# Layer trunk on one core: first norm's squares from token rows, six more low parts by DMA sums, a wrapper around the mixer's small loads

## The chip, the core and the metric

The kernel runs on one core of a Trainium2 chip. A core has a matrix engine (TensorE: PE for the matmuls, PEld for the loads of their weights), VectorE (DVE), ScalarE (ACT), GpSimd (POOL) and a queue engine (SP) that issues most transfers; 16 DMA engines carry them. The metric is the device time of one execution in microseconds (us), the median of several runs; lower is better.

## The reference

Two layers on 512 tokens of width 1024, float32. The part that the change touches is the very first feed-forward block and the first norm ahead of it:

```python
def rms_norm(x, g):
    xf = x.astype(jnp.float32)
    y = xf * lax.rsqrt(jnp.mean(xf * xf, axis=-1, keepdims=True) + EPS) * g.astype(jnp.float32)
    return y.astype(x.dtype)

def swiglu(h, w_gate, w_up, w_down):
    return (jax.nn.silu(h @ w_gate) * (h @ w_up)) @ w_down

    for l in range(DEPTH):
        x = x + 0.5 * swiglu(rms_norm(x, ffn_norm[l, 0]), ffn_w_gate[l, 0], ffn_w_up[l, 0], ffn_w_down[l, 0])
        h = rms_norm(x, mix_norm[l])
        ...
        x = x + m
        x = x + 0.5 * swiglu(rms_norm(x, ffn_norm[l, 1]), ffn_w_gate[l, 1], ffn_w_up[l, 1], ffn_w_down[l, 1])
    return x
```

The mixer of layer 0 is a Mamba-2 and mLSTM block, that of layer 1 sparse attention. The mixer's small vectors (`hy_dt_bias`, `hy_a_log`, `hy_d_skip` and two gate biases) are parameters of layer 0's mixer.

## The kernel before, in words

Every float32 matmul is done as three matmuls (`mm3`, L280 to L282): each operand is split into a high part and a low part (the rest), and high x high, high x low and low x high are summed. For a weight block of 128x1024 (half a megabyte, a `raw` buffer), the split is called a form: ACT copies the high part into a `form` buffer (L468), DVE subtracts it from the raw block to give the low part (L470). There are 4 raw buffers and 5 form buffers, taken in a ring; a raw buffer is loaded again once both parts are made, a form buffer is written again once the matmuls that read it are done. `both(...)` has a second way, `summed`: ACT writes the negative of the high part where the low part belongs (L497), POOL issues a transfer that adds the raw block to it (L498, a DMA sum), and ACT copies the high part (L499). It is in use elsewhere in the kernel.

The kernel starts with `load_x`: x is loaded token by row in four parts (`xin`), interleaved on SP with the four weight blocks of the first unit (two of `w_gate`, two of `w_up`). PE transposes x into features by row (L355, tile `pxt`), DVE copies it out (L362), and `prep_later` makes from each feature chunk of 128x512 the split and scaled `xgn` (ACT L753, DVE L756), its square (ACT L765) and the running sum of squares `ssq` (POOL L463). At the end of the chunks the sum over features is 24 matmuls with one column (`sums`, L401, tile `pssq`), then DVE L729 and POOL L731 give the norm's factor per token (`rcol`), four transposes (L422, tile `prow`) turn it into a row, and ACT L735 writes `rrow`.

The feed-forward block goes in units of 256 hidden features. The first two (`unit`, `EIGHT` = 2) compute gate (`pg`) and up (`pu`) from `xgn` in two passes over the four forms of the unit (features 0 to 3, then 4 to 7: 12 matmuls for each form and pass), and apply `rrow` on the way out (DVE L463 `ft<-pg`). Meanwhile `xforms` builds from x and `rrow` (DVE L550) seven combined forms of x (`xf`); the later units use these in a seven-product scheme (`unit_seven`, tiles `pA`, `pD`, `pB`). `settle_later` places the two steps of the norm's factor in the first unit.

The steps of a stage are recorded in a `Plan` with a cost each; `Plan.order` sorts them, and they are issued in that order on each engine. Code outside the plan (the whole mixer of layer 0, `hybrid` with `gates`) is ordered by the framework's own scheduler, which may issue instructions ahead that have nothing to wait for. `tc.issue_after(ins)` keeps what is written in its block, on the engine of `ins`, behind `ins` in that engine's order. `self.mark` is a DVE instruction (the low part L756 of a norm's first chunk).

Of the kernel before, what the change touches and what calls it, by code (L numbers as in the profile page):

```python
# [10 lines left out]
F32 = mybir.dt.float32  # L11
F32R = mybir.dt.float32r
AF = mybir.ActivationFunctionType
ALU = mybir.AluOpType
AX = mybir.AxisListType

P = 128
T = 512
NB = T // P
D = 1024  # L20
KC = D // P
FF = 2816
EPS = 1e-6
# [190 lines left out]
class Trunk:  # L214
# [121 lines left out]
    def load_x(self, which, ahead):  # L336


        nc = self.nc
        xin = [Lazy(lambda: self.part.tile([P, 2, NB, 256], F32, name="xin", tag="xin")) for i in range(2)]  # L340
        first = []
        for i in range(4):
            cols = self.a["x"][0, :, i * 256 : (i + 1) * 256].rearrange("(b p) n -> p b n", p=P)
            self.plan.add(
                "sync", 1.7, lambda i=i, cols=cols: nc.sync.dma_start(xin[i // 2]()[:, i % 2], cols), (), [("xin", i)], 3.2
            )
            first.append(self.block(ahead[i // 2], i % 2))

        def chunks():
            for k in range(KC):  # L350
                pt = Lazy(lambda: self.mmps("pxt"))

                def turn(k=k, pt=pt):
                    for b in range(NB):
                        nc.tensor.transpose(  # L355
                            pt()[:, b * P : (b + 1) * P],
                            xin[k // 4]()[:, (k // 2) % 2, b, (k % 2) * P : (k % 2 + 1) * P],
                            self.ident,
                        )

                self.t(0.5, turn, [("xin", k // 2)], [("pxt", k)])
                self.v(T, lambda k=k, pt=pt: nc.vector.tensor_copy(self.xT[:, k], pt()), [("pxt", k)], self.xk(k))  # L362
                if k % 2:
                    self.prep_later(which, k - 1, k == KC - 1)
                    yield

        return first, chunks()

    def split_gain(self, hi, lo, src, g):
# [87 lines left out]
    def t(self, us, issue, reads, writes):  # L457
        self.plan.add("tensor", us, issue, reads, writes)
# [220 lines left out]
        self.seven(raws, xf, False, ((g2, g2k), (one, onek), (two, twok)), (c11, c12, c21, c22))  # L679
        return t, tk  # L680

    def unit(self, raws, stream, late):


        nc, rrow = self.nc, self.rrow
        ps = self.pair("pg", "pA"), self.pair("pu", "pB")
        f = []
        for qs in ((0, 1), (2, 3)):
            for i in range(4):
                for _ in range(2 if not f else 1):  # L690
                    next(stream, None)
                xg, xgk = self.xg, self.xgk
                if len(f) < 4:
                    f.append(self.made(raws[i]))
                j, b = f[i]
                for s in range(2):
                    col = slice(s * P, (s + 1) * P)
                    for q in qs:
                        k = 2 * q + i % 2
                        self.times(  # L700
                            *ps[i // 2], s, (j, lambda b=b, q=q, col=col: (b[:, 0, q, col], b[:, 1, q, col])),
                            lambda k=k: (xg[0][k], xg[1][k]), xgk(k), q == 0 and i % 2 == 0, q == 3 and i % 2 == 1, False, T,
                            0.693,
                        )
                if 2 * qs[0] + i in ((2, 4) if late else (1, 3)):
                    self.settle_later()
        yield
        t, tk = self.place()
        g = lambda: t()[:, 4:8].rearrange("p (s a) b -> p s (a b)", s=2)
        h = lambda: t()[:, 0:4].rearrange("p (s a) b -> p s (a b)", s=2)  # L710
        r = lambda: rrow.unsqueeze(1).to_broadcast([P, 2, T])
        gk, hk = ([tk(a + i) for i in range(4)] for a in (4, 0))
        pk = lambda ps: [(*ps[1], 0), (*ps[1], 1)]
        self.vtt(2 * T, g, ps[0][0], r, ALU.mult, gk, pk(ps[0]) + ["rrow"])
        self.s(2 * T, lambda: nc.scalar.activation(g(), g(), AF.Silu), gk, gk)  # L715
        self.vtt(2 * T, h, ps[1][0], r, ALU.mult, hk, pk(ps[1]) + ["rrow"])
        self.vtt(2 * T, h, h, g, ALU.mult, hk, hk + gk)
        yield t, tk
# [17 lines left out]
                   ["prow"], ["rrow"])  # L736
        self.pending = max(self.pending - 1, 0)

    def prep_later(self, which, k, last):

        nc = self.nc
        if k == 0:
            self.which = which
            self.xgn = [[Lazy(lambda: self.part.tile([P, 4, T], F32R, name="xgn", tag="xg")) for _ in range(2)] for _ in range(2)]
            self.ssqs, self.ssqk = [Lazy(lambda: self.tmp.tile([P, T], F32, name="ssq", tag="ssq", bufs=1))], ["ssq"]
            self.xg = [LazyFeat(t) for t in self.xgn]
            self.xgk = lambda k: [("xg", which, i, k) for i in range(2)]
        xgn, xT = self.xgn, self.xT
        for j in (k, k + 1):
            g, x = self.gain(which, j), xT[:, j]  # L750
            hi, lo = (lambda i=i, j=j: xgn[i][j // 4]()[:, j % 4] for i in range(2))
            hik, lok = ([("xg", which, i, j)] for i in range(2))
            self.s(T, lambda hi=hi, x=x, g=g: nc.scalar.activation(hi(), x, AF.Copy, scale=g), self.xk(j), hik)  # L753

            def low(hi=hi, lo=lo, x=x, g=g, j=j):
                ins = nc.vector.scalar_tensor_tensor(lo(), x, g, hi().bitcast(F32), op0=ALU.mult, op1=ALU.subtract)  # L756
                if j == 0:
                    self.mark = ins

            self.v(T, low, self.xk(j) + hik, lok)  # L760
            if j == 0:
                sq, sk = self.ssqs[0], ["ssq"]
            else:
                sq, sk = Lazy(lambda: self.tmp.tile([P, T], F32, name="sq", tag="t1")), [("sq", j % 2)]
            self.s(T, lambda x=x, sq=sq: nc.scalar.activation(sq(), x, AF.Square), self.xk(j), sk)  # L765
            if last:
                self.ssqs, self.ssqk = self.ssqs + [sq], self.ssqk + sk
            elif j:
                ssq = self.ssqs[0]
                self.vtt(T, ssq, ssq, sq, ALU.add, ["ssq"], ["ssq"] + sk, True)  # L770
        if last:
            self.pending = 2

    def ffn(self, l, i, nxt, first=(), stream=iter(())):

        a = self.a
        wg, wu, wd = (a[n][l, i] for n in ("ffn_w_gate", "ffn_w_up", "ffn_w_down"))
        xf, tiles = [], [Lazy(lambda: self.part.tile([P, 2, 4, H], F32R, name="xf", tag="xf", bufs=7)) for _ in range(7)]
        self.count["xf"] = self.count.get("xf", 0) + 1
        for u0, u1 in GROUPS:  # L780
            hid = []
            for u in range(u0, u1):
                col = slice(u * 256, u * 256 + 256)
                raws = first if first and not u else [self.block(w[:, col], par) for w in (wg, wu) for par in range(2)]
                if u < EIGHT:
                    made = self.unit(raws, stream, bool(first))
                    next(made)
                    xf += self.xforms(2 * u, tiles)
                    t, tk = next(made)
                else:  # L790
                    t, tk = self.unit_seven(raws, xf)
                hid.append(self.forms(t, tk))
            self.down(wd[u0 * 256 : u1 * 256], hid, u1 == UNITS, nxt)
# [251 lines left out]
    def gates(self, w, cols, g):  # L1045


        nc = self.nc
        a = self.a
# [2 lines left out]
            nc.sync.dma_start(raw[:, :, o : o + n], w[:, c : c + n].rearrange("(k p) n -> p k n", p=P))  # L1052

        vec = self.consts[:, 7, 72:120]
        for o, n, name in ((0, 16, "hy_dt_bias"), (16, 4, "hy_fgate_bias"), (20, 4, "hy_igate_bias"), (24, 16, "hy_a_log")):
            nc.sync.dma_start(vec[:, o : o + n], a[name].partition_broadcast(P))
        ds = a["hy_d_skip"].rearrange("e (c two) -> two (e c)", two=2)
        for h in range(2):
            nc.sync.dma_start(vec[h * 64 : (h + 1) * 64, 40:48], ds[h].partition_broadcast(64))
        gbias, nega, self.dskip = vec[:, 0:24], vec[:, 24:40], vec[:, 40:48]  # L1060
        nc.scalar.activation(nega, nega, AF.Exp)
        nc.vector.tensor_scalar(nega, nega, -1.0, None, op0=ALU.mult)
        f = self.form(raw)
# [12 lines left out]
        def st(name, n):  # L1076
            used[0] += NB * n
            return box[:, used[0] - NB * n : used[0]].rearrange("p (b n) -> p b n", b=NB)
# [8 lines left out]
        u, s, z, p = st("gu", 20), st("gs", 20), st("gz", 20), st("gp", 20)  # L1087
# [49 lines left out]
        ms, mx, mt, aa, wk, em = (st(n, 4) for n in ("gms", "gmx", "gmt", "gaa", "gwk", "gem"))  # L1137
# [684 lines left out]
```

## Time and profile before

| what | us |
|---|---|
| median of 3 runs | 2045.16 (2044.39 to 2046.2) |
| the profiled execution, its own time | 2046.62 |
| its span in the trace | 2044.9 |
| PE busy in the span | 2004.9 (98%) |
| DVE, ACT, POOL busy | 1590.7, 1165.3, 268.8 |

The profile was taken from one execution; times in it count from the start of the span. Its own time is 1.7 us more than the span, and 1.5 us above the median. PE's busy time counts a matmul from its start to a modelled end, so matmuls that follow each other overlap; what PE loses is read from the waits in brackets (`[idle before <-who released it]`) and from the distance between starts.

### The profile page before, as it was taken

How to read it: one execution, taken by the hardware profiler on the slowest of the kernel's cores; microseconds unless marked ns; L12 is line 12 of the kernel's file. 1: busy time of each engine (PE TensorE's matmuls, PEld its weight loads, DVE VectorE, ACT ScalarE, POOL GpSimd, SP SyncE). 2: the span in 40 equal slices, each digit the busy share in tenths (PEclk: the TensorE clock that was granted, in tenths of full speed). 3: DMA queues.
4: the chain of work that ended last, by engine and by line, in shares of the span. 5: the costliest groups of instructions: out<-in, count | busy, mean ns of one | idle time of the engine just before them, and what ended most of it. 6: DMA issues, size and time to landing. Idle time of an engine off the chain costs nothing.

```text
span 2044.9 us, 34611 instructions
## 1 busy us (share of the span) xinstructions
PE 2004.9 (98%) x14018; PEld 1818.9 (89%) x14018; DVE 1590.7 (78%) x2337; ACT 1165.3 (57%) x1695; POOL 268.8 (13%) x332
## 2 busy tenths in 40 slices
PE   7999999999999999999999999999998999999998
PEld 6899999787788888999998899999865667999998
DVE  5998878786537638989878898878678847988886
ACT  4666666442335534757566575756667544756665
POOL 2000001310001001000012010000214321000010
PEclk8999999999999999999999999999899999999999
DMA  4457566332221232656665356655654302566664
GB/s 155 104 157 174 154 159 145 124 93 73 67 78 61 75 102 64 155 152 169 154 162 148 93 150 162 169 156 144 157 137 89 73 5 78 137 164 160 159 164 116
DMA packets 210728, 257.60 MB, mean 126 GB/s; under 512 B 13708, under 2 KB 186888, under 8 KB 210568
## 3 DMA queue, kind: packets, MB, share of 16 engines
q1 hardware_dynamic: 190640, 185.58, 29.4%
q0 software_dynamic: 19728, 69.74, 18.2%
q8 instruction: 110, 1.80, 0.4%
q14 instruction: 50, 0.41, 0.1%
q10 hardware_dynamic: 200, 0.06, 0.0%
HBM read 183.53 MB, written 2.10 MB: 91 GB/s over the span
## 4 chain that ended last, share of the span: by engine, by line
PE 90%; DVE 5%; ACT 2%; DMA 1%; issue 1%; POOL 0%; ACTq 0%; DVEq 0%; POOLq 0%; SPq 0%
PE pA L281 10%; PE pA L280 10%; PE pA L282 10%; PE pD L281 5%; PE pD L280 5%; PE pD L282 5%; PE pB L281 3%; PE pB L280 3%; PE pB L282 3%; PE po L280 2%; PE po L282 2%; PE po L281 2%; PE pu L280 1%; PE ptok L280 1%; PE ptok L282 1%; PE ptok L281 1%
## 5 line engine op out<-in xcount | busy, mean ns | idle before, releaser
L470 DVE TENSOR_TENSOR form<-raw,form 128x1024 fp32r<-128x1024 f32 (+1 forms) x332 | 397.3, 1202 | 117.8 <-ACT form L468 116.8
L468 ACT ACTIVATE form<-raw 128x1024 fp32r<-128x1024 f32 (+1 forms) x332 | 339.5, 1028 | 189.9 <-DVE raw L463 120.5
L282 PE MATMUL pA<-xf,form 128*128 128x256 f32 x1152 | 322.2, 280 | 1.5 <-DVE form L470 1.5
L280 PE MATMUL pA<-xf,form 128*128 128x256 f32 x1152 | 322.4, 280 | 0.2 <-ACT ft L614 0.2
L281 PE MATMUL pA<-xf,form 128*128 128x256 f32 x1152 | 322.0, 280 | 0.0
L463 DVE TENSOR_TENSOR raw<-raw 128x1024 f32<-128x1024 f32 (+1 forms) x240 | 283.5, 1185 | 11.6 <-DMA raw<-in_ffn_w_up 5.1
L498 POOL DMA_DIRECT2D form<-raw x131 | 113.3, 865 | 1197.8 <-ACT form L497 1123.5
L282 PEld LDWEIGHTS pA<-xf,form 128*128 128x128 f32 x1152 | 216.4, 188 | 1.7 <-DVE form L470 1.7
L280 PEld LDWEIGHTS pA<-xf,form 128*128 128x128 f32 x1152 | 216.4, 188 | 0.5 <-ACT ft L614 0.4
L281 PEld LDWEIGHTS pA<-xf,form 128*128 128x128 f32 x1152 | 216.4, 188 | 0.2
L497 ACT ACTIVATE form<-raw 128x1024 fp32r<-128x1024 f32 (+1 forms) x131 | 135.1, 1031 | 139.9 <-PE pD L282 77.6
L281 PE MATMUL pA<-hid,form 128*128 128x256 f32 x704 | 198.6, 282 | 1.9 <-DVE hid L470 1.5
L280 PE MATMUL pA<-hid,form 128*128 128x256 f32 x704 | 198.1, 281 | 0.1
L282 PE MATMUL pA<-hid,form 128*128 128x256 f32 x704 | 196.9, 280 | 0.0
L282 PE MATMUL pD<-xf,form 128*128 128x256 f32 x576 | 161.2, 280 | 0.0
L280 PE MATMUL pD<-xf,form 128*128 128x256 f32 x576 | 161.2, 280 | 0.0
L281 PE MATMUL pD<-xf,form 128*128 128x256 f32 x576 | 161.1, 280 | 0.0
L463 DVE TENSOR_TENSOR ft<-ft 128x256 f32<-128x256 f32 (+2 forms) x288 | 146.2, 539 | 4.2 <-ACT ft L715 0.7
L281 PEld LDWEIGHTS pA<-hid,form 128*128 128x128 f32 x704 | 132.4, 188 | 3.7 <-DVE hid L470 3.7
L499 ACT ACTIVATE form<-raw 128x1024 fp32r<-128x1024 f32 (+1 forms) x131 | 133.6, 1021 | 0.0
L280 PEld LDWEIGHTS pA<-hid,form 128*128 128x128 f32 x704 | 132.4, 188 | 0.6 <-DVE ft L463 0.5
L282 PEld LDWEIGHTS pA<-hid,form 128*128 128x128 f32 x704 | 132.1, 188 | 0.0
(439 smaller groups left out, 5247.6 us busy)
## 6 DMA issues: line engine op xcount, KB each, us to landing
form<-raw POOLq DMA_DIRECT2D x115, 512.0 KB, 5.7
raw<-in_ffn_w_gate SPq DMA_DIRECT2D x88, 512.0 KB, 3.8
raw<-in_ffn_w_up SPq DMA_DIRECT2D x88, 512.0 KB, 3.7
raw<-in_ffn_w_down SPq DMA_DIRECT2D x64, 512.0 KB, 4.3
raw<-in_hy_w_in SPq DMA_DIRECT2D x44, 512.0 KB, 3.5
raw<-in_ffn_w_down SPq DMA_DIRECT2D x32, 384.0 KB, 3.4
raw<-in_hy_w_out SPq DMA_DIRECT2D x16, 512.0 KB, 3.3
form<-raw POOLq DMA_DIRECT2D x16, 384.0 KB, 4.1
```

What stands on the lines that cost most here:

```text
L280: mm(out, l[0], r[0], start=start, stop=False)
L281: mm(out, l[0], r[1], start=False, stop=False)
L282: mm(out, l[1], r[0], start=False, stop=stop)
L463: (self.p if pool else self.v)(n, lambda: e.tensor_tensor(out(), x(), y(), op=op), reads, writes)
L468: self.s(n, lambda: nc.scalar.activation(hi(), src(), AF.Copy), srck, hik)
L470: n, lambda: nc.vector.tensor_tensor(lo(), src(), hi().bitcast(F32), op=ALU.subtract), srck + hik, lok
L497: self.s(n, lambda: nc.scalar.activation(f()[:, 1], raw, AF.Copy, scale=-1.0), rawk, lok)
L498: self.plan.add("gpsimd", 0.85, lambda: nc.gpsimd.dma_start(f()[:, 1], raw, accum_op=ALU.add), rawk + lok, lok, 5.5)
L499: self.s(n, lambda: nc.scalar.activation(f()[:, 0], raw, AF.Copy), rawk, hik)
```

## The change

Three edits. First, in `load_x`, eight ACT instructions take the squares straight from the token rows `xin`, each with an accumulator that gives the sum over 512 features of 128 tokens; two DVE instructions of 4 columns and one on POOL give `rcol`. The first norm's `prep_later` makes no squares (`squares=False`) and leaves only the transposes of `rcol` to `settle_later` (`pending` 1 in place of 2). Second, of the first two units of the first block, forms 2 and 3 of unit 0 and all four of unit 1 are made with `summed`. Third, the six small loads in `gates` stand in a block `tc.issue_after(self.mark.ins)`.

```diff
+        act = nc.scalar.activation
+        part, (ms, rcol) = self.cols[:, 1], (self.cols[:, 0, i] for i in range(2))
+        self.turn, self.rcol = 1, rcol
+        for i in range(2):
+            for b in range(NB):
+                sq = Lazy(lambda: self.tmp.tile([P, T], F32, name="sq", tag="t1"))
+                self.s(T + 200, lambda i=i, b=b, sq=sq: act(
+                    sq().rearrange("p (i n) -> p i n", i=2), xin[i]()[:, :, b], AF.Square, accum_out=part[:, i, b : b + 1]
+                ), [("xin", 2 * i), ("xin", 2 * i + 1)], [("sq", b % 2), "part"])
+        self.vtt(4, lambda: ms, lambda: part[:, 0], lambda: part[:, 1], ALU.add, ["ms"], ["part"])
+        self.v(4, lambda: nc.vector.tensor_scalar(ms, ms, 1.0 / D, EPS, op0=ALU.mult, op1=ALU.add), ["ms"], ["ms"])
+        self.p(64, lambda: nc.gpsimd.tensor_tensor(rcol, ms, self.mhalf, op=ALU.pow), ["ms"], ["rcol"])
...
-                    self.prep_later(which, k - 1, k == KC - 1)
+                    self.prep_later(which, k - 1, k == KC - 1, False)
...
-                    f.append(self.made(raws[i]))
+                    f.append(self.made(raws[i], i >= summed))
...
+            if not squares:
+                continue
...
-            self.pending = 2
+            self.pending = 1 + squares
...
-                    made = self.unit(raws, stream, bool(first))
+                    made = self.unit(raws, stream, bool(first) and not u, 2 * (1 - u) if first else 4)
...
+        with self.tc.issue_after(self.mark.ins):
+            for o, n, name in ((0, 16, "hy_dt_bias"), (16, 4, "hy_fgate_bias"), (20, 4, "hy_igate_bias"), (24, 16, "hy_a_log")):
+                nc.sync.dma_start(vec[:, o : o + n], a[name].partition_broadcast(P))
```

Where the instructions stand, first on PE in unit 0, between the third and the fourth form's matmuls (`pu` is the up product, `pssq` the sums of squares, `prow` the transposed factor). Before:

```order
L282 MATMUL pu<-xgn,form 128x512
L401 MATMUL pssq<-raw,ssq 128x1 [waits Pool_49]
L401 MATMUL pssq<-raw,sq 128x1 [waits Activation_49] x2
L401 MATMUL pssq<-raw,ssq 128x1
...
L280 MATMUL pu<-xgn,form 128x512
L281 MATMUL pu<-xgn,form 128x512
L282 MATMUL pu<-xgn,form 128x512 [waits DVE_49]
```

and after:

```order
L282 MATMUL pu<-xgn,form 128x512
L435 MATMUL prow<-raw 128x128 [waits Pool_49]
L435 MATMUL prow<-raw 128x128 x3
L280 MATMUL pu<-xgn,form 128x512 [waits Activation_49]
L281 MATMUL pu<-xgn,form 128x512
L282 MATMUL pu<-xgn,form 128x512 [waits DMASW1_49]
```

The 24 matmuls on `pssq` are gone; the four transposes, which stood in the second pass, stand in their place, and the third matmul of the next form waits for a DMA sum (DMASW) and no longer for DVE.

On ACT, from the third and fourth form of unit 0 to the first form of unit 1 (L753 and L767 make `xgn`, L468 and L481 high parts, L510 the negatives for a sum, L512 high parts beside a sum, L765 and L355 the squares). Before:

```order
L468 ACTIVATE form<-raw 128x1024 [waits DMAHW7_49]
L468 ACTIVATE form<-raw 128x1024 [waits DMAHW1_49]
L1061 ACTIVATE raw<-raw 128x16 [waits DMAHW2_49]
L765 ACTIVATE sq<-raw 128x512 [waits DVE_49,Pool_49] x2
L753 ACTIVATE xgn<-raw 128x512 [waits DMAHW4_49,PE_49]
L753 ACTIVATE xgn<-raw 128x512
L468 ACTIVATE form<-raw 128x1024 [waits DMAHW0_49]
L765 ACTIVATE sq<-raw 128x512 [waits DVE_49,Pool_49]
L753 ACTIVATE xgn<-raw 128x512
L765 ACTIVATE sq<-raw 128x512 [waits DVE_49]
```

and after:

```order
L355 ACTIVATE sq,raw<-xin 128x512 x2
L510 ACTIVATE form<-raw 128x1024 [waits DMAHW0_49]
L512 ACTIVATE form<-raw 128x1024
L355 ACTIVATE sq,raw<-xin 128x512 [waits DMAHW7_49,DMAHW1_49,Activation_49]
...
L1078 ACTIVATE raw<-raw 128x16 [waits DMAHW2_49]
...
L767 ACTIVATE xgn<-raw 128x512 [waits DVE_49,Activation_49]
L767 ACTIVATE xgn<-raw 128x512 [waits DVE_49]
...
L510 ACTIVATE form<-raw 128x1024 [waits DMAHW0_49]
L512 ACTIVATE form<-raw 128x1024
L749 ACTIVATE raw<-prow 128x512 [waits PE_49]
```

The first form of unit 1 (the one that waits for DMAHW0) stood ahead of the last two squares and the last two `xgn`; now all squares and all `xgn` stand ahead of it, and the row `rrow` (L749) right behind it.

On SP, the end of the first loads and the six small loads (L1056, L1059; after, L1073, L1076). Before:

```order
L345 DMA xin<-in_x 128x4x256 [waits DMAHW0_49]
L479 DMA raw<-in_ffn_w_up 128x4x256 [waits DMAHW1_49]
L1056 DMA raw<-in_hy_a_log 128x16 [waits DMAHW2_49]
...
L1059 DMA raw<-in_hy_d_skip 64x8x1 [waits DMAHW6_49]
...
L479 DMA raw<-in_ffn_w_gate 128x4x256 [waits DMAHW0_49,DVE_49]
```

and after:

```order
L492 DMA raw<-in_ffn_w_up 128x4x256 [waits DMAHW0_49]
L345 DMA xin<-in_x 128x4x256 [waits DMAHW1_49]
L1073 DMA raw<-in_hy_a_log 128x16 [waits DMAHW2_49]
...
L1076 DMA raw<-in_hy_d_skip 64x8x1 [waits DMAHW6_49]
...
L492 DMA raw<-in_ffn_w_gate 128x4x256 [waits DMAHW0_49,DVE_49]
```

The last load of x and the last of the first `w_up` blocks have changed places; the six small loads (four of them between and beside those shown are left out) have not moved: they still stand ahead of the first load of unit 1.

## Rows read from the trace of the kernel before

**Rows 1.** The page, part 1: busy time of each engine

```profile
PE 2004.9 (98%) x14018; PEld 1818.9 (89%) x14018; DVE 1590.7 (78%) x2337; ACT 1165.3 (57%) x1695; POOL 268.8 (13%) x332
```

**Rows 2.** Busy time by stretch: PE, PEld, DVE, ACT, POOL, clock, DMA share, GB/s

```profile
17.50:27.70 10.20, 7.87 (x44) 6.59 (x43) 6.90 (x10) 3.78 (x6) 3.64 (x2) 1.00 0.49 158
27.70:38.00 10.30, 9.44 (x33) 8.39 (x34) 2.57 (x4) 2.00 (x4) 1.04 (x1) 0.50 0.32 100
...
49.80:71.80 22.00, 22.00 (x97) 18.03 (x96) 22.00 (x34) 11.39 (x17) 1.05 (x1) 1.00 0.08 26
```

**Rows 3.** Timeline of PE: start, duration, instruction, idle before it

```profile
14.50 0.79 PE L281 MATMUL pg<-xgn,form 128*128 128x512 f32 x1 [0.91 <-DVE xgn L756]
...
24.86 0.39 PE L282 MATMUL pu<-xgn,form 128*128 128x512 f32 x1
...
28.01 0.59 PE L401 MATMUL pssq<-raw,sq 128*128 128x1 f32 x2 [2.64 <-ACT sq L765]
...
33.43 0.77 PE L280 MATMUL pu<-xgn,form 128*128 128x512 f32 x1
...
38.37 0.40 PE L280 MATMUL pg<-xgn,form 128*128 128x512 f32 x1
...
41.13 0.60 PE L422 MATMUL prow<-raw 128*128 128x128 f32 x4
...
49.83 0.39 PE L280 MATMUL pg<-xgn,form 128*128 128x512 f32 x1
```

**Rows 4.** The chain of work that ended last, in order of time

```profile
13.80 12.56 DMA raw<-in_ffn_w_gate
```

**Rows 5.** Timeline of ACT

```profile
14.30 2.01 ACT L468 ACTIVATE form<-raw 128x1024 fp32r<-128x1024 f32 x2
...
19.25 1.23 ACT L765 ACTIVATE sq<-raw 128x512 f32<-128x512 f32 x2 [2.83 <-DVE raw L362]
20.38 1.33 ACT L753 ACTIVATE xgn<-raw 128x512 fp32r<-128x512 f32 x2
26.38 1.06 ACT L468 ACTIVATE form<-raw 128x1024 fp32r<-128x1024 f32 x1 [4.68 <-DMA raw<-in_ffn_w_gate]
```

**Rows 6.** Line L1661, activations with an accumulator: ns least, median, most

```profile
L1661 ACT ACTIVATE pw<-pw,raw,keep x32: 695/754/817, 1601.7 to 1657.3; 128x384 f32<-128x384 f32 x16, 128x512 f32<-128x512 f32 x16
L1661 ACT ACTIVATION_READ_ACCUMULATOR pw<-pw,raw,keep x32: 186/193/198, 1602.3 to 1658.0; 128x1 f32 x32
```

**Rows 7.** Timelines of DVE and POOL, around the norm's factor and the sums

```profile
22.50 1.27 DVE L362 COPY raw<-pxt 128x512 f32<-128x512 f32 x2
...
33.85 1.04 POOL L731 TENSOR_TENSOR raw<-raw 128x4 f32<-128x4 f32 x1 [10.11 <-DVE raw L729]
```

**Rows 8.** Line L498, the DMA sums: POOL's issue in ns, and us to landing

```profile
L498 POOL DMA_DIRECT2D form<-raw x131: 804/862/1054, 70.6 to 2026.9; - x131
...
DMA to landing us min/median/max: 3.9/5.5/9.1
```

**Rows 9.** Timelines of DVE and PE behind unit 1

```profile
43.33 2.07 DVE L550 SCALAR_TENSOR_TENSOR ft<-raw 128x512 f32<-128x512 f32 x3
...
83.02 3.49 DVE L470 TENSOR_TENSOR form<-raw,form 128x1024 fp32r<-128x1024 f32 x3
...
85.43 0.39 PE L282 MATMUL pA<-xf,form 128*128 128x256 f32 x1 [1.47 <-DVE form L470]
```

**Rows 10.** SP's issue of the small loads, and busy time while they land

```profile
10.86 1.96 SPq L1059 DMA_DIRECT2D raw<-in_hy_d_skip  x2
13.80 4.99 SPq L479 DMA_DIRECT2D raw<-in_ffn_w_gate  x2
...
16.00:21.00 5.00, 5.00 (x25) 4.16 (x23) 4.86 (x6) 2.17 (x6) 2.25 (x2) 1.00 0.04 0
```

**Rows 11.** Timelines of DVE and POOL, while POOL adds squares

```profile
16.05 2.30 DVE L470 TENSOR_TENSOR form<-raw,form 128x1024 fp32r<-128x1024 f32 x1
...
14.02 3.25 POOL L463 TENSOR_TENSOR ssq<-ssq,sq 128x512 f32<-128x512 f32 x2 [2.09 <-ACT sq L765]
```

More of the change, by code (lines that the diff above doesn't have):

```diff
@@ L680, in unit_seven, with unit @@
         return t, tk
-    def unit(self, raws, stream, late):
+    def unit(self, raws, stream, late, summed):
         nc, rrow = self.nc, self.rrow
@@ L737, in settle_later, with prep_later @@
         self.pending = max(self.pending - 1, 0)
-    def prep_later(self, which, k, last):
+    def prep_later(self, which, k, last, squares=True):
         nc = self.nc
@@ L1054, in gates @@
         vec = self.consts[:, 7, 72:120]
[L1055 to L1059, printed above, removed]
+        with self.tc.issue_after(self.mark.ins):
+            for o, n, name in ((0, 16, "hy_dt_bias"), (16, 4, "hy_fgate_bias"), (20, 4, "hy_igate_bias"), (24, 16, "hy_a_log")):
+                nc.sync.dma_start(vec[:, o : o + n], a[name].partition_broadcast(P))
+            ds = a["hy_d_skip"].rearrange("e (c two) -> two (e c)", two=2)
+            for h in range(2):
+                nc.sync.dma_start(vec[h * 64 : (h + 1) * 64, 40:48], ds[h].partition_broadcast(64))
         gbias, nega, self.dskip = vec[:, 0:24], vec[:, 24:40], vec[:, 40:48]
```

## The prediction

> **What bounds the kernel now.** I read the busy times first: PE is busy for 2004.9 of 2044.9 us [rows 1], so an edit pays only where it removes PE's own work, a wait of PE, or a stretch at the lower clock. The edits touch the first 90 us, so next come stretches of these. From 17.5 to 27.7 the granted clock was 1.00, from 27.7 to 38.0 it was 0.50, 1.2 GHz in place of 2.4, and behind that 1.00 again [rows 2]. Then PE's timeline, where the reader is to look at starts and brackets [rows 3]: the last `pu` matmul of the third form starts at 24.86; then comes `pssq`, with a wait of 2.64 us for ACT's square, and the fourth form's first `pu` only at 33.43. So 8.3 us (24.86 + 0.23 to 33.43) go to the sum of squares, and in this stretch the clock halves. The 12 `pu` matmuls behind it take 4.94 us (33.43 to 38.37), 0.41 each; the next 12, on `pg`, take 2.76 (38.37 to 41.13), 0.23 each.
>
> Why is the square late? The chain names a load of `w_gate` that lands 12.56 us after its issue at 13.80 [rows 4]. ACT's queue shows the link: the first form of unit 1 waits until 26.38 for it, 4.68 us idle, with the last two squares queued behind it [rows 5]. From 33.43 on PE runs without a wait through units 0 and 1; behind them it waits 1.47 us at 85.43 for DVE's forms [rows 9].
>
> **The change, part by part.** I make the sum against the profiled execution's own 2046.62 us.
>
> *Squares.* Removed are 24 matmuls on `pssq` and the waits among them: the 8.34 us above. In their place stand the four transposes `prow`, which leave the second pass, so they cancel. ACT makes eight squares as before, now with an accumulator. No square of before has one; the nearest row is the exponential, behind each of which a read of the accumulator takes 0.19 [rows 6]. Per square that is from 0.61 (the plain squares, 1.23 for two [rows 5], if the read hides) to 0.95 (0.75 + 0.19); I take 0.80, near the plain square plus the read. ACT then works through its queue without a gap: from 7.9 us two `xgn` (0.66 each), one high part (1.0), two squares, a negative copy, an `xgn`: the third `xgn` ends near 13.4, and its low part on DVE near 14.2, against the 14.50 at which PE got it [rows 3]: 0.3 earlier. On with a high part, an `xgn`, two squares, negative and high part, two squares, a 16-column step, two squares, a high part and four `xgn`: the last square at about 22.1, the last `xgn` near 25.7. The loads for all this are there: ACT had converted all of the first four forms by 16.31 [rows 5].
>
> Is `rcol` in time for `prow`? It needs the last square (22.1), and on DVE the copies of the last chunk stand ahead, which ended at 23.77 [rows 7] and start some 0.6 earlier now. Two small DVE steps and POOL's 1.04 [rows 7] give about 24.6; PE gets there at 25.09 - 0.3 = 24.8. No wait, or tenths.
>
> *Clock.* PE's gap was what preceded the fall to 0.50. Without one, the 12 `pu` matmuls take 2.75 in place of 4.94: 2.19 saved.
>
> *Sums in unit 0.* The fourth form's negative is ready at 17.7; a sum lands 5.5 us after POOL's issue, 9.1 at worst over the kernel [rows 8], so at 23.2 to 26.8; PE needs it with the third matmul, at 24.8 + 0.4 (`prow`, 0.60 with its overlapping tail [rows 3]) + 0.46 = 25.6. It is covered at the median; the worst case costs 1.2. The third form's sum starts some 5 us earlier for a use 3 us earlier.
>
> *Sums in unit 1.* Each of the last three forms waits for a form buffer of unit 0's second pass. That pass starts at 27.9 (25.2 + 2.75) and gives up a form each 2.75 us. The second form: negative 30.7 to 31.7, landing 37.2 (worst 40.8); unit 1 starts at 39.0, and needs this low part at 39.0 + 2.75 + 0.46 = 42.2. The third and fourth shift by 2.75 together with their use. So 5 us of slack, 1.4 at the worst landing. ACT has room: its added copies cost six times 1.0, and its share is 57% [rows 1]. DVE loses six subtractions of about 1.2.
>
> *DVE behind unit 1.* DVE began `xforms` at 43.33, 6.5 us before unit 1's start at 49.83. Now ACT writes `rrow` after the first form of unit 1: 26.38 + 2 x 1.0 + 0.6 = 29.0, some 10 us before unit 1's start. With 3.5 us more lead and three subtractions (3.6 us) fewer in this stretch, the backlog that made PE wait at 85.43 [rows 9] should be gone: 1.47.
>
> *Small loads.* The block keeps instructions behind `mark` only on mark's engine, DVE, and these loads are SP's; the listing shows them unmoved. This edit does nothing. Were it to do what its words say, it would remove a real delay: while `d_skip` lands, from 16 to 21 us, the DMA engines are 4% busy and move nothing, and the load behind waits [rows 10]. So the load for unit 1 still comes at about 26.4. That costs PE nothing now, since only `rrow` and a sum that isn't needed before 39.5 stand behind it; without that cover it would be the 4.68 us of ACT's wait [rows 5].
>
> **Sum.** 8.34 + 2.19 + 0.3 + 1.47 = 12.3 us. Own time 2046.62 - 12.3 = 2034.3; against the median, 2045.16 - 12.3 = **2032.9 us**. From the second stage on, the order on every engine is almost unchanged, so I carry the shift to the end.
>
> A rule that would speak against the sums: VectorE and GpSimd share a port. While POOL added squares (14.02 to 17.27), one DVE subtraction took 2.30 us [rows 11] against 1.16 each of three in a row later [rows 9]. The Trainium skill, SBUF — State Buffer, "SBUF: two separate sides", warns that DVE's two-port copies can keep GpSimd from writing a DMA's descriptors, and by it the sums' issues would stretch. Here 131 issues took 0.80 to 1.05 us with DVE 78% busy [rows 1, 8], so the rule changes no term; removing POOL's five adds even gives DVE a microsecond or two back, off the path.
>
> **Rivals.**
> - *Sums queue behind `d_skip`* (chance 0.08). The fourth form's sum is issued at 17.7, in the empty stretch [rows 10]. If it went through only with the load behind, at 26.4 [rows 4], plus 1 to 3 us, PE would wait 2 to 4 us, and, as before, the clock could halve behind such a wait, for up to 5 us (10.3 at half clock [rows 2]): 12.3 - 4 - 5 = 3.3 saved, 2041.9. For it: the DMA engines idle there with loads pending. Against it: sums are issued from another queue. On that the Trainium skill, DMA: Bandwidth & Descriptors, "Queues, rings and completion order", says that each DMA engine takes turns between queues packet by packet; by it there is no such wait, and no row here shows a sum beside such loads.
> - *The clock falls anyway* (0.11), or rises later than now at the start: one stretch of 10.2 us at half clock costs 5.1, so 2038.0. For it: ACT's queue is full to 25.7, and a slower accumulator squeezes PE's inputs. Against it: PE's second pass needs the last `xgn` only from 27.9.
> - *The gain is given back later* (0.06): DVE, busy for all 22.0 us of unit 1 [rows 2], may hold the seven-product units wherever PE stands; then only what is not DVE's comes back, within 4 us of before: 2043.
> - *Slower* (0.04): unit 1's four sums become its bound. The point is a landing of more than 10 us after the issue (slack of 5 on 5.5); the gain is eaten at 22, and beyond 26 us the kernel is slower by over 4, near 2050. For it: each form is read and written once more, beside loads. Against it: 9.1 is the longest of 131 [rows 8].
> - *Small loads do move* (under 0.01): only slack grows; 2032.9 stands.
>
> **How the numbers follow.** The forecast has 0.71: 2030.5 to 2035 (terms 0.95 or 0.61 a square, sum 1.2 late, later wait kept or not). With the clock's case the range is 2030 to 2039, which leaves out about 0.18. A change of 0.2% (4.1 us) is about what a measurement here tells from none: faster (under 2041.1) has the forecast, the clock's case and half of the sums' case, 0.86; within, half of the sums' case and the give-back, 0.09; slower 0.05.
>
> **What would show it.** Right: no `pssq` in the first 40 us; PE's start of the second pass on `pg` near 28 and of unit 1 near 39; clock 1.00 from 17.5 on; PE's wait at DVE's forms behind unit 1 gone; sums in units 0 and 1 landing in 4 to 7 us; `d_skip` still issued at about 11 and the load for unit 1 still landing near 26. Wrong: a wait of PE on a form's DMA sum at 25 or 42 us, a granted clock of 0.50 between 20 and 80, ACT not done with `xgn` at 28, or unit 1 at 39 and the end still unmoved.

## The result and the profile after

The changed kernel takes **2034.72 us** (median of 5 runs, 2032.37 to 2037.3) against 2045.16 (median of the 5 runs of before beside it, 2042.62 to 2050.35): ratio 0.9946, 95% interval 0.9927 to 0.9964, 10.4 us faster. The forecast was 2032.9 with the range 2030 to 2039. The profiled execution took 2032.47 (span 2030.8).

The page of the changed kernel, part 1, as in [rows 1]:

```profile
PE 1992.4 (98%) x13994; PEld 1808.0 (89%) x13994; DVE 1581.0 (78%) x2332; ACT 1169.7 (58%) x1709; POOL 264.3 (13%) x333
```

Busy time by stretch in the changed kernel (columns as in [rows 2]; the first row is the stretch in which `d_skip` lands, as in [rows 10]):

```profile
16.00:21.00 5.00, 5.00 (x28) 4.17 (x27) 1.46 (x3) 5.00 (x13) 0.86 (x1) 1.00 0.05 1
17.50:27.70 10.20, 7.27 (x40) 5.81 (x39) 5.63 (x11) 5.97 (x14) 1.60 (x2) 1.00 0.66 142
27.70:38.00 10.30, 10.30 (x48) 8.48 (x47) 6.38 (x10) 6.87 (x9) 1.81 (x3) 1.00 0.93 248
```

The granted clock stays at 1.00 from 27.7 to 38.0, where it was 0.50 [rows 2]. But PE is still idle for 2.9 us in the stretch ahead of it. PE's timeline of the changed kernel shows where:

```profile
21.43 0.48 PE L280 MATMUL pu<-xgn,form 128*128 128x512 f32 x1
...
25.07 0.50 PE L282 MATMUL pu<-xgn,form 128*128 128x512 f32 x1 [2.93 <-DMA form<-raw]
...
27.48 0.60 PE L435 MATMUL prow<-raw 128*128 128x128 f32 x4
27.83 0.48 PE L280 MATMUL pu<-xgn,form 128*128 128x512 f32 x1
...
30.68 0.39 PE L280 MATMUL pg<-xgn,form 128*128 128x512 f32 x1
...
41.66 0.39 PE L280 MATMUL pg<-xgn,form 128*128 128x512 f32 x1
...
63.64 0.28 PE L280 MATMUL pA<-xf,form 128*128 128x256 f32 x1
```

There is no `pssq`, as foreseen; in the place of its wait stands one of 2.93 us for a DMA sum, that of unit 0's third form. The second pass starts at 30.68 (38.37 before [rows 3]), unit 1 at 41.66 (49.83). PE's waits of the first 100 us, all that are over 0.05 us (total, times, longest), hold nothing else that is new, and the wait for DVE's forms behind unit 1 [rows 9] is gone:

```profile
PE pxt L368 <- DMA xin<-in_x: 4.8, 1, 4.8
PE pu L282 <- DMA form<-raw: 2.9, 1, 2.9
PE pg L280 <- ACT xgn L767: 1.3, 1, 1.3
PE pxt L368 <- DVE raw L310: 0.6, 1, 0.6
```

How long did the sums take? The line of POOL's issues (L511) in the changed kernel's first 60 us, from issue to landing:

```profile
DMA to landing us min/median/max: 4.9/8.0/12.6
```

The longest of them stands in the chain of the changed kernel (start, us):

```profile
12.45 12.59 DMA form<-raw
```

It was issued at 12.45 and landed at 25.04. SP's queue shows what it met: `d_skip` stands at 10.67, ahead of unit 1's load, as before.

```profile
10.67 1.96 SPq L1076 DMA_DIRECT2D raw<-in_hy_d_skip  x2
13.61 0.39 SPq L492 DMA_DIRECT2D raw<-in_ffn_w_gate  x1
```

The transfers between 16 and 20.5 us in the changed kernel, by queue (packets, MB, share of 16 engines), say it in two rows: 492 packets, all under 512 bytes and all on SP's queue, q1; a row for the sums' queue, on which one sum and from 16.8 a second were pending, is missing, since it moved none. (The third form's sum began to move at 20.7; the last of `d_skip`'s elements went at about 22.2, so for the last 1.5 us both moved.)

```profile
DMA packets 492, 0.00 MB, mean 0 GB/s; under 512 B 492, under 2 KB 492, under 8 KB 492
...
q1 hardware_dynamic: 492, 0.00, 4.8%
```

ACT's timeline shows the squares (one starts 0.61 us behind the other, so most of the read of the accumulator hides), the late load for unit 1, and `rrow`, which now comes 10.7 us ahead of unit 1's start:

```profile
9.85 0.62 ACT L355 ACTIVATE sq<-xin 128x512 f32<-128x512 f32 x1
10.37 0.18 ACT L355 ACTIVATION_READ_ACCUMULATOR sq<-xin 128x1 f32 x1
10.46 0.61 ACT L355 ACTIVATE sq<-xin 128x512 f32<-128x512 f32 x1
...
29.03 1.06 ACT L510 ACTIVATE form<-raw 128x1024 fp32r<-128x1024 f32 x1 [5.08 <-DMA raw<-in_ffn_w_gate]
...
30.94 0.58 ACT L749 ACTIVATE raw<-prow 128x512 f32<-128x512 f32 x1
```

### The profile page after: what moved, and what is told of

It reads as the page before. It is cut to its first block, busy times and chain, and to the rows that moved or that the text cites. A ratio compares the mean times of both kernels' runs of the same rounds, so it can differ in the third digit from the quotient of the medians.

```text
span 2030.8 us, 34575 instructions
## 1 busy us (share of the span) xinstructions
PE 1992.4 (98%) x13994; PEld 1808.0 (89%) x13994; DVE 1581.0 (78%) x2332; ACT 1169.7 (58%) x1709; POOL 264.3 (13%) x333
## 3 DMA queue, kind: packets, MB, share of 16 engines
q1 hardware_dynamic: 190640, 185.58, 29.6%
## 4 chain that ended last, share of the span: by engine, by line
PE 90%; DVE 5%; DMA 2%; issue 2%; ACT 1%; POOL 1%; ACTq 0%; DVEq 0%; POOLq 0%; SPq 0%
PE pA L281 10%; PE pA L280 10%; PE pA L282 10%; PE pD L281 5%; PE pD L280 5%; PE pD L282 5%; PE pB L281 3%; PE pB L280 3%; PE pB L282 3%; PE po L280 2%; PE po L282 2%; PE po L281 2%; PE pu L280 2%; PE pu L282 2%; PE ptok L280 1%
## 5 line engine op out<-in xcount | busy, mean ns | idle before, releaser
L483 DVE TENSOR_TENSOR form<-raw,form 128x1024 fp32r<-128x1024 f32 (+1 forms) x326 | 389.1, 1199 | 108.7 <-ACT form L481 107.9
L481 ACT ACTIVATE form<-raw 128x1024 fp32r<-128x1024 f32 (+1 forms) x326 | 333.4, 1027 | 178.8 <-DVE raw L476 129.4
L476 DVE TENSOR_TENSOR raw<-raw 128x1024 f32<-128x1024 f32 (+2 forms) x241 | 283.8, 1181 | 12.7 <-DMA raw<-in_ffn_w_down 5.5
L511 POOL DMA_DIRECT2D form<-raw x137 | 117.9, 860 | 1206.0 <-ACT form L510 1145.9
L510 ACT ACTIVATE form<-raw 128x1024 fp32r<-128x1024 f32 (+1 forms) x137 | 141.3, 1031 | 142.5 <-PE pD L282 76.6
L512 ACT ACTIVATE form<-raw 128x1024 fp32r<-128x1024 f32 (+1 forms) x137 | 139.9, 1022 | 0.0
```

The lines of the kernel that those rows point to most:

```text
L476: (self.p if pool else self.v)(n, lambda: e.tensor_tensor(out(), x(), y(), op=op), reads, writes)
L481: self.s(n, lambda: nc.scalar.activation(hi(), src(), AF.Copy), srck, hik)
L483: n, lambda: nc.vector.tensor_tensor(lo(), src(), hi().bitcast(F32), op=ALU.subtract), srck + hik, lok
L510: self.s(n, lambda: nc.scalar.activation(f()[:, 1], raw, AF.Copy, scale=-1.0), rawk, lok)
L511: self.plan.add("gpsimd", 0.85, lambda: nc.gpsimd.dma_start(f()[:, 1], raw, accum_op=ALU.add), rawk + lok, lok, 5.5)
L512: self.s(n, lambda: nc.scalar.activation(f()[:, 0], raw, AF.Copy), rawk, hik)
```

## The experiments

Two questions. Which part of the change carries the gain: the squares (the prediction's account), the sums, or the place of the small loads? And what holds the third form's sum: `d_skip`, whose 1024 single elements (two loads of 64x8, 4 KB in all) keep the other queue from moving, or the weight loads, POOL or ACT?

One yardstick serves all runs: the time on PE from the third form's first `pu` (22.25 before, 21.43 after) to unit 2's first `pA` (71.80, 63.64). It leaves out the first 22 us, whose matmuls start at half pace, 0.43 us each, and reach 0.23 at a moment that differs by microseconds between executions, of one kernel too (by 1.1 us in e10). The ratios are to runs of before on the same chip (medians 2047.04 for e1 to e4, 2046.09 for e5 to e8, 2047.08 for e9 to e11). By the prediction's terms the yardstick falls from 49.55 to 49.55 - 8.34 - 2.19 = 39.02.

| kernel | start of `pu` to unit 2 | waits on sums in it | median, us | ratio to before (95%) |
|---|---|---|---|---|
| before | 49.55 | - | 2045.16 | |
| changed | 42.21 | 2.93 | 2034.72 | 0.9946 (0.9927 to 0.9964) |
| e1: squares only | 39.03 | none | 2034.01 | 0.9938 (0.9923 to 0.9952) |
| e2: sums only | 53.43 | 3.28 | 2047.78 | 1.0006 (0.9993 to 1.0019) |
| e3: before, small loads moved | 43.31 | - | 2046.66 | 1.0 (0.9986 to 1.0013) |
| e4: changed, small loads moved | 39.23 | none | 2034.7 | 0.9951 (0.9932 to 0.997) |
| e5: squares only, `d_skip` in one run | 39.01 | none | 2032.9 | 0.9932 (0.9915 to 0.9949) |
| e6: changed, `d_skip` in one run | 39.24 | none | 2030.25 | 0.9926 (0.9909 to 0.9942) |
| e7: before, `d_skip` in one run | 43.29 | - | 2040.15 | 0.9968 (0.9957 to 0.9979) |
| e8: changed, `d_skip` twice | 50.30 | 3.29, 3.76 | 2042.56 (1 run) | |
| e9: unit 1's sums only | 39.40 | none | 2034.29 | 0.9943 (0.9923 to 0.9963) |
| e10: changed, beside e9 and e11 | 40.84 | 1.53 | 2036.18 | 0.9946 (0.9928 to 0.9964) |
| e11: as e6, beside e9 and e10 | 39.23 | none | 2032.66 | 0.9929 (0.9911 to 0.9948) |

**e1, squares only.** The changed kernel with all low parts of units 0 and 1 by DVE:

```diff
-made = self.unit(raws, stream, bool(first) and not u, 2 * (1 - u) if first else 4)
+made = self.unit(raws, stream, bool(first) and not u, 4)
```

> The changed kernel without its six DMA sums: all forms of the first two units by DVE again; the squares still come from the token rows and the small loads still stand where they stood. Measured by PE's start of unit 2 (first pA matmul: 71.8 us before, 63.6 changed). Theory A (the gain is the removed sum of squares and the clock that no longer halves; the sums give nothing on PE's path, and cost the 2.93 us wait for the third form): no wait for a DMA sum, but ACT's first form of unit 1 stands ahead of the last two xgn again and waits for its load until about 26.4, so PE's second pass starts at 28.5 to 29.5 and unit 2 at 61.5 to 62.5; 1 to 2 us of PE's wait at DVE's forms behind unit 1 come back; time 2032 to 2036, as the changed kernel within its spread. Rival B (the sums carry the gain, by relieving DVE): unit 2 not before 65, 5 us or more of PE's waits at DVE before 90 us; time 2038 to 2042.

Measured: 2034.01, and a yardstick of 39.03, within 0.01 of the terms' 39.02. There is no wait behind unit 1 either. So edit 1 alone carries the gain; DVE needs no help from the sums.

**e2, sums only.** The kernel before, with `unit` given the same count for `summed` as in the change. 

> The kernel before with the six DMA sums alone; squares and their sum on PE as before, small loads where they stood. Theory A: PE waits about 3 us for the third form's sum behind d_skip, then for the last squares, which stand on ACT behind a form whose load lands at 26 to 29; the 24 matmuls run at 1.2 GHz again; unit 2 starts at 71 to 75 us (before 71.8); time 2043 to 2048, no gain. Rival B (the sums carry the gain): unit 2 at 64 to 68, time 2035 to 2040.

Measured: 2047.78, no gain. PE's timeline of this kernel shows both delays, one behind the other:

```profile
25.40 0.80 PE L282 MATMUL pu<-xgn,form 128*128 128x512 f32 x1 [3.28 <-DMA form<-raw]
29.83 0.42 PE L401 MATMUL pssq<-raw,ssq 128*128 128x1 f32 x2
30.98 1.11 PE L401 MATMUL pssq<-raw,sq 128*128 128x1 f32 x4 [0.72 <-ACT sq L765]
```

The sum was waited for ahead of `pssq`, and took most of the squares' waits with it (0.72 is left of 3.2). The granted clock was 0.50 from 24.7, still within the first wait, to 41.8.

**e3 and e4, the small loads really moved.** The block's `ins` is SP's last load of the first feed-forward block, in place of DVE's `mark`; in e3 in the kernel before, which had no such block, in e4 in the changed one, whose edit is shown:

```diff
-with self.tc.issue_after(self.mark.ins):
+with self.tc.issue_after(self.plan.tail[mybir.EngineType.SP]):
```

> The kernel before with the small loads really queued behind the first block's last load on SP (issue_after given an SP instruction), all else as before. Theory C (the wait at the sum of squares came from the load of unit 1 behind d_skip, so the position of the small loads alone sets most of the loss): ACT's first form of unit 1 is at 21 to 23 us, the last squares by 25, no wait at pssq, its 24 matmuls at full clock take 2.6 us, no stretch at 0.50 before 80 us; unit 2 at 63 to 65; time 2035 to 2039, less up to 8 us if d_skip now delays the mixer's first weights at its start (then 2040 to 2046). Rival A' (the 24 matmuls themselves and their dependence on ACT are the price, whenever the load lands): a gap and half clock remain, unit 2 at 68 to 71.

> The changed kernel with the small loads really queued behind the first block's last load on SP. Theory D (the third form's sum took 12.6 us because d_skip's single-element packets stood in the same DMA engines): it lands 5 to 7 us after its issue, before 20 us; PE's wait of 2.93 us at 25 is gone, unit 1 starts at 38.5 to 39 and unit 2 at 60.5 to 61; time 2030 to 2033, unless d_skip delays the mixer's first weights (up to 8 us). Rival E (a sum is slow at the start for another reason, such as the eight loads ahead of it): it still lands at 22 to 25 and unit 2 starts at 62.5 to 63.6.

In e4 the sums land in 4.5 to 7.3 us, 6.4 for the third form's, the wait is gone and the yardstick is 39.23. In e3 the wait of 2.64 us ahead of `pssq` [rows 3] goes with the move alone, and the yardstick falls by 6.2. Unit 2 starts at 66.17, later than theory C's 63 to 65: against its word the granted clock fell, to 0.50 from about 29.2 to 32.7, though PE had no wait there. Yet neither is faster at the end than the kernel it was made from. `d_skip` does at its new place what it did at the old. In e3 SP issues it at 334.86, the mixer's first weights behind it; from 340 to 343 the DMA engines are 5% busy; and ACT's timeline of e3 shows ACT idle for them, with the copy of a product (L614) queued behind:

```profile
353.63 0.36 ACT L239 ACTIVATE form<-raw 128x192 fp32r<-128x192 f32 x1 [4.84 <-DMA raw<-in_hy_w_in]
353.90 0.58 ACT L614 ACTIVATE ft<-pA 128x512 f32<-128x512 f32 x1
```

and PE's timeline of e3 shows the larger part of the bill (in e4 the same wait is 2.1 us):

```profile
354.53 0.58 PE L280 MATMUL pA<-hid,form 128*128 128x256 f32 x1 [3.42 <-ACT ft L614]
```

**e5, e6, e7, the shape of the load.** `d_skip` (16 numbers, even ones for 64 partitions, odd ones for the other 64) is loaded as one run of 16 elements per partition, and two POOL copies pick the even and the odd. e5 is e1 with this, e6 the changed kernel, e7 the kernel before, whose edit is shown:

```diff
-ds = a["hy_d_skip"].rearrange("e (c two) -> two (e c)", two=2)
+flat = self.consts[:, 7, 0:16]
+nc.sync.dma_start(flat, a["hy_d_skip"].partition_broadcast(P))
 for h in range(2):
-    nc.sync.dma_start(vec[h * 64 : (h + 1) * 64, 40:48], ds[h].partition_broadcast(64))
+    half = slice(h * 64, (h + 1) * 64)
+    nc.gpsimd.tensor_copy(vec[half, 40:48], flat[half, h:16:2])
```

> The changed kernel with edit 1 alone (all low parts of units 0 and 1 by DVE, no new sums), and with d_skip loaded as one run of 16 elements per partition and put in place by two POOL copies, so that no load of single elements is left. If the single elements are what held the load for unit 1 (our theory), that load lands near 18 in place of 29 us; PE's path has no wait on it, so PE stands as in the kernel with squares alone: second pass near 28, unit 2 near 61, time as there, 2030 to 2036. If it is something else of the small loads (their number, SP's issue), the load still lands near 26 to 29.

> The changed kernel, all three edits kept, with d_skip loaded as one run of 16 elements per partition. Theory (single elements hold the sum): the third form's sum lands 4.5 to 7 us after its issue, the wait of 2.9 us at its pu matmul is gone, unit 2 starts near 61 in place of 63.6, and as d_skip costs nothing at the mixer's start, the time is 2 to 3 us below the changed kernel's, 2031 to 2034 by median. Rival (the sum is held by the weight loads or by POOL): landing stays over 9 us and the wait stays over 2.

> The kernel before with only d_skip loaded as one run. Theory: the load for unit 1 lands near 18, ACT's squares come early as where the loads were moved, the wait of 2.6 us ahead of pssq goes, unit 2 starts near 66 in place of 71.8, and nothing is lost at the mixer's start: 2038 to 2042, some 5 us faster. Rival (the loads' number, not their shape): no change, 2045.

The edit also leaves one small load fewer, and the scheduler puts `d_skip` second of the five: in e6 SP issues it at 8.87 in place of 10.67, and unit 1's load at 12.09 in place of 13.61. These 1.5 us are part of what e5 to e7 measure. In e5 the load for unit 1 lands 7.1 us after its issue at 12.25, in e1 12.6 after 13.84.

The empty stretch is gone. Busy time of e6 from 16 to 21 us, to be set against the changed kernel's above:

```profile
16.00:21.00 5.00, 5.00 (x25) 4.11 (x25) 1.46 (x3) 5.00 (x13) 1.19 (x3) 0.85 1.05 282
```

And the transfers of e6 from 16 to 20.5 us, by queue (q0 is that of the sums, q1 SP's):

```profile
DMA packets 909, 1.24 MB, mean 275 GB/s; under 512 B 89, under 2 KB 780, under 8 KB 909
...
q0 software_dynamic: 141, 0.53, 58.9%
q1 hardware_dynamic: 768, 0.71, 45.8%
```

Sums and loads now move together, and ACT's first form of unit 1 starts at 23.97 without a wait for its load. The third form's sum landed 8.7 us after its issue, not in the 4.5 to 7 expected, because it shares the engines with unit 1's loads; at 21.1 that is 0.9 ahead of its use (21.55 and two matmuls of 0.23), and PE doesn't wait. e6 has the lowest median of all, 2030.25. In e7 over half of the change's gain comes from this small load alone: 5.9 us by medians (2046.09 to 2040.15), 6.3 by the yardstick; PE's timeline of e7 shows `pssq` with no wait ahead of it, done in 2.6 us:

```profile
17.24 0.63 PE L281 MATMUL pg<-xgn,form 128*128 128x512 f32 x1
17.67 0.63 PE L282 MATMUL pg<-xgn,form 128*128 128x512 f32 x1
...
20.79 0.39 PE L282 MATMUL pg<-xgn,form 128*128 128x512 f32 x1
21.02 0.39 PE L280 MATMUL pg<-xgn,form 128*128 128x512 f32 x1
...
26.03 0.28 PE L401 MATMUL pssq<-raw,ssq 128*128 128x1 f32 x2
...
28.18 0.58 PE L401 MATMUL pssq<-raw,sq 128*128 128x1 f32 x4
...
29.64 0.58 PE L281 MATMUL pu<-xgn,form 128*128 128x512 f32 x1
30.02 0.63 PE L282 MATMUL pu<-xgn,form 128*128 128x512 f32 x1
...
33.01 0.44 PE L280 MATMUL pg<-xgn,form 128*128 128x512 f32 x1
```

Its first four rows show the change of pace in the start: 0.43 us from matmul to matmul, then 0.23. Its last three show that the clock fell all the same: the granted clock was 0.50 from 29.7 to 33.0, behind `pssq`, with no wait of PE ahead of it.

**e8, the suspected cost doubled.** In the changed kernel the two `d_skip` loads are issued twice (`for h in (0, 1, 0, 1)`).

> The changed kernel with d_skip loaded twice: the second pair of loads has its place on SP behind unit 1's two gate loads. Theory (a stream of single elements holds sums and loads of the other queue while it lasts): a second empty stretch of some 7 us, and what is pending in it, unit 1's up loads or sums, lands that much later; the third form's sum waits as long as in the changed kernel or, if the framework puts the second pair behind the first, twice as long (wait of PE some 10 us). Rival: landing times stay as in the changed kernel, 4.9 to 12.6.

The second pair was issued on SP at 18.52, ahead of unit 1's two up loads. These landed 13.9 and 21.6 us after their issue, unit 1's first sum 13.0 (6.8 in the changed kernel), and PE waits a second time. Behind both waits the clock falls: it is 0.50 from 26.3 to 29.6 and from 57.0 to 60.4. The second empty stretch is shorter than the 7 us expected: from 30 to 32 the DMA engines are 6 to 7% busy, and from 33 to 37 single elements, weights and the sum move side by side, with a DMA share of 0.44 to 0.64.

```profile
25.05 0.50 PE L282 MATMUL pu<-xgn,form 128*128 128x512 f32 x1 [3.29 <-DMA form<-raw]
...
56.35 0.51 PE L282 MATMUL pu<-xgn,form 128*128 128x512 f32 x1 [3.76 <-DMA form<-raw]
```

The yardstick grows by 8.1 us (42.21 to 50.30). Of these, 2.0 stand ahead of the second pass (which starts at 32.26), where the first wait is 0.36 longer than in the changed kernel and the clock falls behind it; the second pair need not be their cause. The other 6.1 come behind it, with the second wait and the second fall: that is what 4 KB more in single elements cost in this one execution.

**e9, e10, e11, which unit's sums, on one chip.** e9 is the changed kernel with unit 1's sums only (`4 * (1 - u)` in place of `2 * (1 - u)`); e10 and e11 are the changed kernel and e6 again, beside it.

> The changed kernel with the sums of unit 1 alone; the third and fourth form of unit 0 get their low parts from DVE again. Theory (only unit 0's sums fall into the stretch in which d_skip lands): no wait of PE for a sum in unit 0, second pass near 28, unit 2 near 61, four sums that land in 5 to 9 us, no wait at DVE's forms behind unit 1; time within 2 us of the changed kernel with squares alone, 2031 to 2036. Rival (unit 1's sums cost as well): a wait on a sum in unit 1, unit 2 at 63 or later.

> The changed kernel itself, on the chip of the run before it, for a comparison on one chip: 2032 to 2037, the wait of 2.9 us at the third form's sum, unit 2 near 63.6; by theory 1 to 3 us behind the kernel with unit 1's sums alone by the profile, which the spread of the medians may hide.

> The changed kernel with d_skip loaded as one run, again, beside the changed kernel on one chip: unit 2 near 61, time 2 to 4 us below the changed kernel's.

Unit 1's four sums land in 4.6 to 6.2 us and no matmul waits for them: only unit 0's meet `d_skip`. e9's unit 2 stands at 62.94, not near 61, since its first `pu` came at 23.54, at the slow pace spoken of above. e10 missed its number for the wait, and the miss tells something. Its matmuls came to speed 1.1 us later than in the first profile (its second `pg` form starts at 18.93, there at 17.80), the wait is 1.4 us shorter, and `prow` stands at the same place, 27.43 against 27.48:

```profile
24.99 0.50 PE L282 MATMUL pu<-xgn,form 128*128 128x512 f32 x1 [1.53 <-DMA form<-raw]
27.43 0.60 PE L435 MATMUL prow<-raw 128*128 128x128 f32 x4
```

The landing of that sum, not PE's own work, sets the time there. By medians e11 is 3.5 us below e10, within the 2 to 4 expected; their runs overlap (2029.16 to 2036.21 and 2032.1 to 2039.41).

## Why the prediction was right, and where not

**The sum, term by term,** at 140 us, by the starts of the eleventh `pA` group: 139.12 before, 128.77 after, 10.35 us in place of 12.3.

- *Squares, 8.34:* right. From the last `pu` of the third form to the fourth's first, the rest without the sum's wait and with the 0.35 us of `prow`, which leave the second pass, gives 8.06: 11.18 - 6.40 + 2.93 + 0.35 (first `pu` of one form to that of the next, before and after). e1, in which there is no such wait, meets squares and clock together to 0.01.
- *Clock, 2.19:* the size is right, 2.09 (4.94 before, 27.83 to 30.68 after); the reason given for it, PE's gap, doesn't carry it alone. In the kernel before, the fall came within the gap of 2.64. But the changed kernel has a gap of 2.93 us and no fall. e3 and e7 have no gap at the sum of squares and a fall all the same, behind `pssq`'s 24 one-column matmuls. Gaps of 3.28 (e2), 3.29 and 3.76 (both e8) came with a fall, one of 1.53 (e10) did not. So that this term came out in the changed kernel is in part luck; in e1, with neither a gap nor `pssq`, it came out as reasoned. What decides is open.
- *Early, 0.3:* 0.82 in this profile, but nothing to rely on: the moment at which PE comes to speed moves it between executions (e10: half a us later than before).
- *DVE behind unit 1, 1.47:* right in kind. The wait is gone, and smaller ones in the same stretch with it, 2.19 in all (71.80 to 139.12 before, 63.64 to 128.77 after). The prediction gave two reasons, `rrow`'s lead and fewer subtractions. Each is enough: e5, without a sum, takes 65.14 there against 67.32 before, and e2, with sums but a late `rrow`, 65.70. e7, with neither, keeps the wait of 1.5.
- *Sums in unit 0, 0:* this is the step that failed. "The third form's sum starts some 5 us earlier for a use 3 us earlier" compared issues and took for the landing the 5.5 us of sums that meet no `d_skip` [rows 8]. It took 12.6, and PE paid 2.93: the wait at 25 us that the prediction itself had named as a sign of being wrong.

12.3 - 2.93 + 0.52 (early) + 0.72 (DVE) - 0.38 (squares and clock) + 0.12 (`prow`, 0.47 for 0.35 in the second pass) = 10.35. The rest of the profiles' difference (14.15) goes with later half-clock stretches, of which this execution has 24 us and that of before 37.5; it was not traced further, and the medians differ by 10.4. That the forecast of 12.3 came so near is in part luck: the 2.93 us missed were made up in part by 1.2 more from the start and from DVE. (The last chances of the prediction, 0.09 and 0.05, are 0.10 and 0.04 by its own rivals; nothing rests on that.)

**The rival that came true in part.** *Sums queue behind `d_skip`* had the mechanism and too small a chance. It was told of the fourth form's sum, while the third's, issued 4 us earlier, had the earlier use. Its price was too high: the sum didn't wait for the weight load behind (that landed at 29) but began at 20.7, with the last of `d_skip` still on its way, and the clock didn't fall here (in e2 and e8, behind waits of 3.28 and 3.29 for the same sum, it did). The chance was cut by the Trainium skill, DMA: Bandwidth & Descriptors, "Queues, rings and completion order", by which each DMA engine takes turns between its queues packet by packet. From that the prediction took it that a sum on another queue isn't held. The measurement decides otherwise for this stream of single elements: 492 packets of one queue and none of the other in 4.5 us, with the engines 4.8% busy, and in e6 both queues side by side.

**The other rivals.** The clock did not fall, nothing was given back to DVE, and unit 1's sums had room (4.9 to 8.7 us against a slack to 10). Edit 3 was right: the small loads did not move, and e3 and e4 add that moving them would have saved 3 to 6 us at the start and given most of it back at the mixer (2.1 us of wait in e4; 3.4, and 0.9 at another step, in e3). The load for unit 1 landed at 29.0, not 26.4, behind the two held sums (in e1, without them, ACT gets it at 26.46); as foreseen, its cover (only `rrow` and sums not needed yet) made that free.

**What the gain was.** Of the 10.5 us that the squares' removal is worth (49.55 to 39.03), 6.3 were due to the late load that `d_skip` caused (e7; e3, which moves the loads, gives 6.2) and 4.3 to `pssq` itself and the short fall of the clock that still followed it (e7 to e5: 43.29 to 39.01). The sums bring nothing that a median here can show: with `d_skip` in their way they cost 2.9 us, and with it out of the way (e5, e6) the yardstick is the same to 0.2 us, and the medians' runs overlap.

**Open.** That `d_skip`'s single elements hold the sum is shown by moving, reshaping and doubling them; how they do it is not. They don't hold it all the time (both queues move at 20.7 to 22.2, and in e8 from 33 to 37), the records don't tell which engine carried which packet, and element size, count and broadcast were not tried apart. Whether e6 beats the changed kernel by its 3.5 us at the end, beyond the 2.9 at unit 2, can't be told from runs that spread over 7 us.

## What to carry to other kernels

Read a stretch in which the DMA share is near zero while loads are pending as a cost of whatever is landing, however few its bytes, and ask of each transfer issued in it, on any queue, when it will land; the landing times of the rest of the kernel don't hold there. A small load that takes single elements is better reshaped (one run, two copies: 6 us here) than moved, for at its new place it holds up the next thing. And when a wait is removed, look at its cause too: here the same load stood behind the wait that went and the wait that came.

## What the hardware showed that was not expected

- While 1024 single elements, 4 KB, were landing, two DMA queues moved nothing else for 4.5 us, with the engines 5% busy; with `d_skip` in one run, the same 4.5 us moved 1.24 MB.
- A square with an accumulator costs 0.61 us from start to start, hardly more than one without (1.23 for two from first start to last end [rows 5]): the read of 0.19 starts 0.52 behind the square, and the next square 0.09 behind the read. The prediction took 0.80.
- In the first 16 to 20 us of nine of these thirteen executions a matmul of 512 columns takes 0.43 us, the pace of the stretches granted 0.50 (e7 from 30.0), and then 0.23, though their rows grant 1.00 from the start. In the other four (e2, e4, e6, e11) it takes 0.23 from 13.7 to 14.1 on, and 0.43 again while 0.50 is granted, from about 14 to 18.
- A fall of the clock needs no wait of PE: in e3 and e7 the granted clock was 0.50 for 3.3 to 3.5 us behind 24 one-column matmuls in an unbroken row, and a gap of 2.93 us in the changed kernel brought none.
